# Step two's adaLN products queued behind the product that spreads the context's rstd, with priority for the context's first block

## Chip, cores and metric

The kernel runs on one core of a Trainium2 chip. The metric is the device time of one execution in microseconds (us). Engines: PE (TensorE, matmuls; PEld is its weight load), DVE (VectorE), ACT (ScalarE), POOL (GpSimd), SP (the engine that issues the loads).

## What is computed

One layer of a diffusion backbone: 256 latent tokens and 256 context tokens with 2048 features, all in float32. The part that matters here is the beginning, the modulated norm of both streams and the products with w_qkv that follow:

```python
sh1, sc1, g1, sh2, sc2, g2 = adaln(cond_lat, w_ada[i], b_ada[i])       # silu(c) @ w + b, 6 parts
h = modulate(rms_norm(x, norm_mix_g[i]), sh1, sc1)                     # x * (1 + scale) + shift
csh1, csc1, cg1, csh2, csc2, cg2 = adaln(cond_ctx, w_ada[i], b_ada[i])
hc = modulate(rms_norm(ctx, norm_mix_g[i]), csh1, csc1)
y, yc = neighbourhood_attention(h, hc, na_w_qkv[j], ..., not last)     # q, k, v = split(t @ w_qkv, 3)
x = x + g1 * y
hf = modulate(rms_norm(x, norm_ffn_g[i]), sh2, sc2)
x = x + g2 * conv_ffn(hf, ffn_w_up[i], ffn_conv_w[i], ffn_conv_b[i], ffn_w_down[i])
```

## The kernel before

Operands lie with features on the partitions, in 16 blocks of 128 features. Every product with a weight matrix is made of three matmuls of rounded halves: high weight with high input (L378), low weight with high input (L379), high weight with low input (L380). The halves of a weight tile are made from the loaded tile `wr`: `wh` on ACT (L163), `wl` on DVE (L164). The halves of the modulated input are `hh` (ACT, L452) and `hl` (DVE, L453).

The kernel begins in steps ("grains"): two steps of one block of features each, then seven of two blocks.

```python
GRAINS = [(0, 1), (1, 1)] + [(k, 2) for k in range(2, 16, 2)]
```

Step one is block 0, step two block 1, step three blocks 2 and 3, step four blocks 4 and 5. For each step `ada_step` makes shift and scale of its blocks for both streams: four groups of adaLN products, here called q0 to q3, each on its own quarter of the rows of w_ada. A group's weights come in two loads (L407) into one of four buffers `wx`; its matmuls (L413) add into a bank `ms`. Then ACT copies the sums to `ev` (L420), PE transposes them (L423), and DVE adds up the quarters and the bias (L428 to L436). `modulate` applies the result to the blocks (L447, L452, L453), and `first_products` multiplies the modulated blocks with the k columns and two groups of v columns of w_qkv. The k products add up in four banks `pj` over all steps; the v products of a step go to one of two banks `mx` and from there to `vsum` (L478 on ACT in step one, L480 on DVE afterwards). The pieces of a step's products are traced between the groups of the next step's `ada_step`.

The norm's rstd is made by `stats`: squares on ACT (L360), sums over the blocks on DVE (L365), sums over the partitions on PE (`col_sums`, L235, into an `mx` bank), rstd on DVE and POOL (L216 to L208), a diagonal matrix `xd` or `cd` (L221), a matmul with ones that spreads rstd over the partitions (L226, into an `mx` bank), and a copy `xb` or `cb` (L228). The latent stream `xl` is loaded and treated first, the context `xc` (L353) during step one: step one's latent products are traced before the context's `stats`, its context products after it.

The order on each engine is chosen by the scheduler of the framework: it plays the program through with estimated times and, whenever an engine is free, takes the ready instruction that was traced first. `tc.high_priority()` makes what is traced within it count as traced earlier. `tc.issue_after(ins)` queues what is traced within it, on the engine of `ins`, behind `ins`; it adds no wait. On the chip every engine works through its list in that order, and so does SP with its loads: a load that waits for its buffer holds up all loads behind it.

Of the kernel before, what the change touches and what calls it, by code (L numbers as in the profile page):

```python
# [15 lines left out]
P = 128  # L16
# [31 lines left out]
GRAINS = [(0, 1), (1, 1)] + [(k, 2) for k in range(2, 16, 2)]  # L48
# [6 lines left out]
def block_kernel(  # L55
# [13 lines left out]
    nc = tc.nc  # L69
# [9 lines left out]
    def ms():  # L79
        return ps.tile([P, CH], F32, tag="ms", name="ms", bufs=2)  # L80

    def mx():
        return ps.tile([P, CH], F32, tag="mx", name="mx", bufs=2)
# [13 lines left out]
    ones = cp.tile([P, P], F32, name="ones")  # L97
# [50 lines left out]

    last = []

    lows = []

    def wpair(src, k0, kn, c0, cn):
# [34 lines left out]
    def ahead():  # L188

        while plan and len(split) < 2:  # L190
            split.append((plan[0], wpair(*plan.popleft())))
# [8 lines left out]
    def rsqrt_newton(pool, v, n, name, bufs=2):  # L200

        r, t = [pool.tile([P, n], F32, tag=name + i, name=name + i, bufs=bufs) for i in "rt"]
        nc.gpsimd.tensor_tensor(out=r, in0=v, in1=mhalf[:, :n], op=ALU.pow)
        nc.vector.tensor_mul(t, r, r)
        nc.vector.scalar_tensor_tensor(
            out=t, in0=t, scalar=-0.5, in1=v, op0=ALU.mult, op1=ALU.mult
        )
        nc.vector.scalar_tensor_tensor(  # L208
            out=r, in0=t, scalar=1.5, in1=r, op0=ALU.add, op1=ALU.mult
        )  # L210
        return r

    def rstd_rows(pool, sums, name, copy):

        v = pool.tile([P, 2], F32, tag=name + "v", name=name + "v")
        nc.vector.tensor_scalar(  # L216
            out=v, in0=sums, scalar1=1.0 / D, scalar2=EPS, op0=ALU.mult, op1=ALU.add
        )
        r = rsqrt_newton(pool, v, 2, name, 1)
        dg = pool.tile([P, 2, P], F32, tag=name + "d", name=name + "d")  # L220
        diag = nc.vector.tensor_tensor(  # L221
            out=dg, in0=ident.unsqueeze(1).to_broadcast([P, 2, P]),
            in1=r.unsqueeze(2).to_broadcast([P, 2, P]), op=ALU.mult,
        )
        bp = mx()[:, :T]
        nc.tensor.matmul(bp, ones, dg.rearrange("p b t -> p (b t)"), start=True, stop=True)  # L226
        rb = pool.tile([P, T], F32, tag=name + "b", name=name + "b")
        copy(rb, bp)  # L228
        return rb, bp, diag.ins

    def col_sums(sums, parts):

        for i, sq in enumerate(parts):
            for b in range(2):
                nc.tensor.matmul(  # L235
                    sums[:, b : b + 1], sq[:, b * P : (b + 1) * P], ones[:, 0:1],
                    start=(i == 0 and b == 0), stop=(i == len(parts) - 1 and b == 1),
                    skip_group_check=True,
                )
        return sums  # L240
# [89 lines left out]
    def hl(kt, t):  # L330
        return hls[kt // (KD // 2)][:, kt % (KD // 2), t]
# [6 lines left out]
    s32 = xp.tile([P, KD, 32], F32, name="s32")  # L338
# [3 lines left out]
    xc = big.tile([P, KD, T], F32, tag="row1", name="xc")  # L342
# [7 lines left out]
    def stream(xin, src):  # L350
        for part in range(4):
            ks = slice(part * KD // 4, (part + 1) * KD // 4)
            nc.sync.dma_start(xin[:, ks, :], src.rearrange("(k p) t -> p k t", p=P)[:, ks, :])  # L353

    def stats(xin, name):

        sacc = None
        for kt in range(0, KD, 2):
            sq = xp.tile([P, 2, T], F32, tag="sq", name="sq", bufs=3)
            nc.scalar.activation(sq, xin[:, kt : kt + 2, :], AF.Square)  # L360
            if sacc is None:
                sacc = sq
            else:
                nacc = xp.tile([P, 2, T], F32, tag="sacc", name="sacc", bufs=2)
                nc.vector.tensor_add(nacc, sacc, sq)  # L365
                sacc = nacc
        sums = col_sums(mx()[:, 0:2], (sacc[:, 0], sacc[:, 1]))
        return rstd_rows(xp, sums, name, nc.vector.tensor_copy)
# [28 lines left out]
    def ada_step(b0, nb, work=()):  # L397

        ap_ = ms()
        n = 2 * nb * P  # L400
        for q in range(4):
            if q < len(work):
                work[q]()
            w = xp.tile([P, 4 * CH], F32, tag="wx", name="wx", bufs=4)[:, : 4 * n]
            for which in range(2):
                c0 = which * D + b0 * P
                load = nc.sync.dma_start(  # L407
                    w.rearrange("p (k s f) -> p k s f", k=4, s=2)[:, :, which, :],
                    w_ada[q * CH : (q + 1) * CH, c0 : c0 + n // 2].rearrange("(k p) f -> p k f", p=P),
                )  # L410
            loads.append(load.ins)
            for k in range(4):
                nc.tensor.matmul(  # L413
                    ap_[32 * k : 32 * k + 32, :n], s32[:, 4 * q + k, :], w[:, k * n : (k + 1) * n],
                    start=(q == 0), stop=(q == 3), tile_position=(0, 32 * k),
                )
        for piece in work[4:]:
            piece()
        ev = xp.tile([P, CH], F32, tag="ev", name="ev")
        nc.scalar.copy(ev[:, :n], ap_[:, :n])  # L420
        sp = ms()
        for b in range(2 * nb):
            nc.tensor.transpose(sp[:, b * P : (b + 1) * P], ev[:, b * P : (b + 1) * P], ident)  # L423
        blk = slice(b0, b0 + nb)
        spv = sp.rearrange("p (b g c) -> p b c g", g=4, c=32)
        for which, dst in ((0, shT), (1, gsT)):
            bcol = S_B + which * KD + b0
            nc.vector.tensor_reduce(  # L428
                out=dst[:, blk, :], in_=spv[:, which * nb : (which + 1) * nb, 0:2, :], axis=AX.X,
                op=ALU.add,  # L430
            )
            nc.vector.tensor_tensor(
                out=dst[:, blk, :], in0=dst[:, blk, :],
                in1=sm[:, bcol : bcol + nb].unsqueeze(2).to_broadcast([P, nb, 2]), op=ALU.add,
            )
        nc.vector.scalar_tensor_tensor(  # L436
            out=gsT[:, blk, :], in0=gsT[:, blk, :], scalar=1.0,
            in1=sm[:, S_GM + b0 : S_GM + b0 + nb].unsqueeze(2).to_broadcast([P, nb, 2]),
            op0=ALU.add, op1=ALU.mult,
        )  # L440

    def modulate(b0, nb, streams=None):

        for st, x_ in streams or ((0, xl), (1, xc)):
            t = slice(st * T, (st + 1) * T)
            for kt in range(b0, b0 + nb):
                nc.vector.scalar_tensor_tensor(  # L447
                    out=x_[:, kt, :], in0=x_[:, kt, :], scalar=gsT[:, kt, st : st + 1], in1=rb[st],
                    op0=ALU.mult, op1=ALU.mult,
                )  # L450
                sh = shT[:, kt, st : st + 1]
                nc.scalar.activation(hh[:, kt, t], x_[:, kt, :], AF.Identity, bias=sh)  # L452
                nc.vector.scalar_tensor_tensor(  # L453
                    out=hl(kt, t), in0=x_[:, kt, :], scalar=sh, in1=hh[:, kt, t].bitcast(F32),
                    op0=ALU.add, op1=ALU.subtract,
                )
# [29 lines left out]

    stream(xl, xT)
    rb = [stats(xl, "x")[0]]
    ada_step(*GRAINS[0])
    ahead()  # L490
    stream(xc, ctxT)
# [1 line left out]
    work = first_products(*GRAINS[0])  # L493
    work[0]()
    work[1]()
    rb.append(stats(xc, "c")[0])
    modulate(*GRAINS[0], ((1, xc),))
    for j, grain in enumerate(GRAINS):
        work = first_products(*grain) if j else work[2:]
        if j + 1 < len(GRAINS):  # L500
            ada_step(*GRAINS[j + 1], work)
            modulate(*GRAINS[j + 1])
        else:
            for piece in work:
                piece()
# [36 lines left out]
    def split_k(kps):  # L542
        kh = kv.tile([P, 4, 2 * T], F32R, tag="kh", name="kh")
        kl = kv.tile([P, 4, 2 * T], F32R, tag="kl", name="kl")
        for tt in range(4):
            norm_transpose(kps[tt], kg, kh, kl, tt * P)
        return kh, kl
# [132 lines left out]
    def out_of_psum(pts, dst):  # L680

        for tt, pt in enumerate(pts):
            nc.scalar.copy(dst[:, tt, :], pt)
        return [dst[:, tt, :] for tt in range(len(pts))]

    k = split_k(out_of_psum(kps, kw))
    q = split_q(out_of_psum(project(0, 2), qw))
    for g in range(3):
# [13 lines left out]
        k = split_k(kps)  # L702
        q = split_q(qps)
# [301 lines left out]
```

## Time and profile before

| | |
|---|---|
| median of 3 runs | 1408.59 us (1408.5 to 1409.4) |
| profiled execution | 1407.63 us |
| its span | 1405.8 us |
| PE busy | 1379.6 us, 98% of the span |
| DVE busy | 1027.2 us, 73% |
| ACT busy | 702.8 us, 50% |
| moved by DMA | 317.14 MB, mean 226 GB/s |

The span runs from the first to the last instruction of the program in the profiled execution; all times of the trace count from its start. The share of busy time is an average over stages; the stage of the change is the first 54 us. The line numbers are those of the kernel before.

### The profile page before, as it was taken

How to read it: one execution, taken by the hardware profiler on the slowest of the kernel's cores; microseconds unless marked ns; L12 is line 12 of the kernel's file. 1: busy time of each engine (PE TensorE's matmuls, PEld its weight loads, DVE VectorE, ACT ScalarE, POOL GpSimd, SP SyncE). 2: the span in 40 equal slices, each digit the busy share in tenths (PEclk: the TensorE clock that was granted, in tenths of full speed). 3: DMA queues.
4: the chain of work that ended last, by engine and by line, in shares of the span. 5: the costliest groups of instructions: out<-in, count | busy, mean ns of one | idle time of the engine just before them, and what ended most of it. 6: DMA issues, size and time to landing. Idle time of an engine off the chain costs nothing.

```text
span 1405.8 us, 20819 instructions
## 1 busy us (share of the span) xinstructions
PE 1379.6 (98%) x7672; PEld 1166.5 (83%) x7672; DVE 1027.2 (73%) x1694; ACT 702.8 (50%) x1218; POOL 54.8 (4%) x57
## 2 busy tenths in 40 slices
PE   4999999999999999999999999999999999999999
PEld 2565788888888888888988888888888888888888
DVE  4555678879877989789897887878878675545454
ACT  4322254564444573554675565655556564333333
POOL 1000010120010020000000000000000000000000
PEclk9999999999999999999999999999999999999999
DMA  9998737768776878656767777777776666566554
GB/s 306 357 354 288 232 95 239 228 214 257 227 243 188 275 209 277 192 189 225 241 187 250 242 227 233 234 238 237 239 238 200 179 190 206 183 208 204 171 178 145
DMA packets 208919, 317.14 MB, mean 226 GB/s; under 512 B 23360, under 2 KB 87744, under 8 KB 208816
## 3 DMA queue, kind: packets, MB, share of 16 engines
q1 hardware_dynamic: 208688, 315.79, 71.8%
q8 instruction: 60, 0.98, 0.3%
q14 instruction: 43, 0.35, 0.1%
q10 hardware_dynamic: 128, 0.01, 0.0%
HBM read 312.75 MB, written 3.01 MB: 225 GB/s over the span
## 4 chain that ended last, share of the span: by engine, by line
PE 94%; DVE 2%; DMA 2%; SPq 1%; issue 0%; ACT 0%; DVEq 0%; ACTq 0%
PE pj L734 20%; PE pj L741 10%; PE mx L734 9%; PE pj L378 8%; PE pj L379 8%; PE pj L380 8%; PE ms L734 8%; PE mx L741 5%; PE ms L741 4%; PE mx L378 2%; PE mx L379 2%; PE ms L413 2%; PE mx L380 2%; DMA wx<-in_w_ada 1%; PE ms L633 1%; DVE wl L164 1%
## 5 line engine op out<-in xcount | busy, mean ns | idle before, releaser
L164 DVE TENSOR_TENSOR wl<-wr,wh 128x1024 fp32r<-128x1024 f32 (+2 forms) x425 | 477.4, 1124 | 254.3 <-ACT wh L163 126.5
L163 ACT CAST wh<-wr 128x1024 fp32r<-128x1024 f32 (+2 forms) x425 | 413.5, 974 | 487.6 <-PE pj L734 127.8
L379 PE MATMUL pj<-wl,hh 128*128 128x512 f32 x512 | 202.6, 396 | 0.0
L380 PE MATMUL pj<-wh,hl 128*128 128x512 f32 x512 | 199.8, 392 | 0.0
L378 PE MATMUL pj<-wh,hh 128*128 128x512 f32 x512 | 193.0, 396 | 2.5 <-ACT hh L452 2.5
L280 DVE SCALAR_TENSOR_TENSOR acc<-wa,sT,acc 128x512 f32<-128x512 f32 x240 | 184.1, 769 | 1.9
L734 PE MATMUL pj<-hf,wh 128*128 128x512 f32 x624 | 146.3, 390 | 0.0
L734 PEld LDWEIGHTS pj<-hf,wh 128*128 128x128 f32 x624 | 115.6, 188 | 23.0
L378 PEld LDWEIGHTS pj<-wh,hh 128*128 128x128 f32 x512 | 95.8, 188 | 26.4 <-issue 3.4
L379 PEld LDWEIGHTS pj<-wl,hh 128*128 128x128 f32 x512 | 96.5, 188 | 21.4 <-DVE wl L164 0.9
L380 PEld LDWEIGHTS pj<-wh,hl 128*128 128x128 f32 x512 | 96.4, 188 | 18.8
L734 PE MATMUL mx<-hf,wh 128*128 128x512 f32 x352 | 94.6, 390 | 0.0
L734 PE MATMUL ms<-hf,wh 128*128 128x512 f32 x336 | 90.5, 389 | 0.0
L741 PEld LDWEIGHTS pj<-hf,wl 128*128 128x128 f32 x624 | 77.5, 192 | 1.6
L741 PE MATMUL pj<-hf,wl 128*128 128x256 f32 x624 | 78.0, 283 | 0.0
L734 PEld LDWEIGHTS mx<-hf,wh 128*128 128x128 f32 x352 | 64.7, 188 | 12.3
L734 PEld LDWEIGHTS ms<-hf,wh 128*128 128x128 f32 x336 | 63.1, 188 | 13.4
L480 DVE TENSOR_TENSOR vsum<-vsum,mx 128x512 f32<-128x512 f32 x64 | 43.1, 683 | 34.3 <-PE mx L380 34.1
L873 ACT ACTIVATE y<-z,sm 128x256 f32<-128x256 f32 x86 | 51.6, 601 | 10.6 <-DVE z L856 10.6
L413 PE MATMUL ms<-wx,s 128*32 128x512 f32 (+1 forms) x288 | 36.9, 582 | 16.3 <-DMA wx<-in_w_ada 16.3
L378 PE MATMUL mx<-wh,hh 128*128 128x512 f32 x128 | 52.7, 412 | 0.1
L379 PE MATMUL mx<-wl,hh 128*128 128x512 f32 x128 | 50.6, 395 | 0.0
(264 smaller groups left out, 2031.7 us busy)
## 6 DMA issues: line engine op xcount, KB each, us to landing
wr<-in_w_up SPq DMA_DIRECT2D x160, 512.0 KB, 4.4
wa<-in_w_ada SPq DMA_DIRECT2D x128, 512.0 KB, 5.0
wr<-in_w_qkv SPq DMA_DIRECT2D x93, 512.0 KB, 4.2
wr<-in_w_down SPq DMA_DIRECT2D x63, 512.0 KB, 4.8
wx<-in_w_ada SPq DMA_DIRECT2D x56, 512.0 KB, 8.8
wr<-in_w_o SPq DMA_DIRECT2D x24, 512.0 KB, 4.9
wr<-in_w_down SPq DMA_DIRECT2D x45, 256.0 KB, 3.1
wr<-in_w_up SPq DMA_DIRECT2D x16, 384.0 KB, 3.9
```

What stands on the lines that cost most here:

```text
L163: a = nc.scalar.copy(hi[:, :kn, :cn], w[:, :kn, :cn])
L164: b = nc.vector.tensor_tensor(out=lo[:, :kn, :cn], in0=w[:, :kn, :cn], in1=hi[:, :kn, :cn].bitcast(F32), op=ALU.subtract,)
L280: nc.vector.scalar_tensor_tensor(out=acc, in0=w[:, k, :], scalar=s, in1=acc, op0=ALU.mult, op1=ALU.add)
L378: nc.tensor.matmul(pt, hh[:, kt, ts], wh[:, k, :], start=a, stop=False)
L379: nc.tensor.matmul(pt, hh[:, kt, ts], wl[:, k, :], start=False, stop=False)
L380: nc.tensor.matmul(pt, hl(kt, ts), wh[:, k, :], start=False, stop=z)
L413: nc.tensor.matmul(ap_[32 * k : 32 * k + 32, :n], s32[:, 4 * q + k, :], w[:, k * n : (k + 1) * n], start=(q == 0), stop=(q == 3), tile_pos ...
L480: nc.vector.tensor_add(acc[:, h0 + i, :], acc[:, h0 + i, :], pr_[i])
L633: nc.tensor.transpose(tp[:, kt * P : (kt + 1) * P], pr[:, kt * P : (kt + 1) * P], ident)
L734: nc.tensor.matmul(pts[b][:, : m.shape[-1]], wh[:, k, bs], m, start=(kt == 0 and t.start == 0), stop=False,)
L741: nc.tensor.matmul(pts[b][:, : m.shape[-1]], wl, m, start=False, stop=(kt == kn - 1))
L873: nc.scalar.activation(y, z, AF.Identity, bias=sm[:, S_CB + f : S_CB + f + 1], scale=sm[:, cw + 1 : cw + 2])
```

## The change

The adaLN products of step two are queued on PE behind the matmul that spreads the context's rstd. The context's `stats` and the modulation of its first block are traced with priority. The end of `ada_step` (copy, transposes, sums) becomes a function of its own, which is traced with priority in step two. The other steps' `ada_step` and all operations stay as they are; the list `behind` is empty in step one and from step three on.

```diff
+    behind = []
...
         bp = mx()[:, :T]
-        nc.tensor.matmul(bp, ones, dg.rearrange("p b t -> p (b t)"), start=True, stop=True)
+        mm = nc.tensor.matmul(bp, ones, dg.rearrange("p b t -> p (b t)"), start=True, stop=True)
+        behind[:] = [mm.ins]
...
             loads.append(load.ins)
-            for k in range(4):
-                nc.tensor.matmul(
-                    ap_[32 * k : 32 * k + 32, :n], s32[:, 4 * q + k, :], w[:, k * n : (k + 1) * n],
-                    start=(q == 0), stop=(q == 3), tile_position=(0, 32 * k),
-                )
+            with ExitStack() as es:
+                for ins in behind:
+                    es.enter_context(tc.issue_after(ins))
+                for k in range(4):
+                    nc.tensor.matmul(
+                        ap_[32 * k : 32 * k + 32, :n], s32[:, 4 * q + k, :],
+                        w[:, k * n : (k + 1) * n], start=(q == 0), stop=(q == 3),
+                        tile_position=(0, 32 * k),
+                    )
         for piece in work[4:]:
             piece()
+        with ExitStack() as es:
+            if b0 == 1:
+                es.enter_context(tc.high_priority())
+            ada_end(ap_, b0, nb)
+
+    def ada_end(ap_, b0, nb):
+
+        n = 2 * nb * P
         ev = xp.tile([P, CH], F32, tag="ev", name="ev")
...
     rb = [stats(xl, "x")[0]]
+    behind.clear()
     ada_step(*GRAINS[0])
...
     work[1]()
-    rb.append(stats(xc, "c")[0])
-    modulate(*GRAINS[0], ((1, xc),))
+    with tc.high_priority():
+        rb.append(stats(xc, "c")[0])
+        modulate(*GRAINS[0], ((1, xc),))
     for j, grain in enumerate(GRAINS):
         work = first_products(*grain) if j else work[2:]
         if j + 1 < len(GRAINS):
             ada_step(*GRAINS[j + 1], work)
+            behind.clear()
             modulate(*GRAINS[j + 1])
```

## The prediction

> **What bounds the kernel now.** I read the page first, then the busy time by stretches, then the chain of waits, then the timeline and the loads of the first 54 us.
>
> ```profile
> span 1405.8 us, 20819 instructions
> PE 1379.6 (98%) x7672; PEld 1166.5 (83%) x7672; DVE 1027.2 (73%) x1694; ACT 702.8 (50%) x1218; POOL 54.8 (4%) x57
> DMA  9998737768776878656767777777776666566554
> ...
> core 0: us, PE busy (x) PEld busy (x) DVE busy (x) ACT busy (x) POOL busy (x), PEclk, DMA share, GB/s
> 28.00:35.30 7.30, 4.57 (x44) 2.21 (x44) 1.98 (x7) 1.52 (x4) 0.70 (x1) 1.00 1.13 320
> 12.00:53.70 41.70, 34.27 (x187) 19.23 (x188) 21.00 (x55) 17.39 (x31) 1.41 (x2) 1.00 1.11 339
> 53.70:142.00 88.30, 88.28 (x452) 55.63 (x452) 51.19 (x103) 22.92 (x36) 0.00 (x0) 1.00 1.00 328
> 142.00:560.00 418.00, 417.87 (x2034) 344.19 (x2034) 338.73 (x586) 205.43 (x459) 48.00 (x39) 1.00 0.72 222
> ```
>
> PE is the bound: busy 88.28 of 88.30 us from 53.7 to 142 and 417.87 of 418.00 after that. So what the change is worth is read before 53.7 us. There the DMA share is 1.11 (full) at 339 GB/s while PE idles 41.70 - 34.27 = 7.4 us, 7.30 - 4.57 = 2.73 of them between 28 and 35.3 us, where the change acts. The chain of waits says on what:
>
> ```profile
> 24.02 0.43 PE pj L379
> ...
> 26.58 0.36 PE mx L379
> ...
> 27.39 0.48 PE mx L380 x2
> 27.87 0.30 SPq L407
> ...
> 28.22 5.42 DMA wx<-in_w_ada
> ...
> 33.77 0.67 PE ms L413 x8
> 34.47 0.38 ACT ev L420
> ...
> 34.90 0.44 PE ms L423 x2
> ...
> 44.47 9.11 DMA wx<-in_w_ada
> 53.58 0.14 issue
> 53.72 1.06 PE ms L413 x8
> ```
>
> Columns: start, duration, what. Twice the chain runs through a load of w_ada: the last one of step two (landed at 33.64) and the load issued at 44.47, which lands at 53.58 and releases step four's first products at 53.72. The stretch's own instructions:
>
> ```profile
> 22.68 0.49 ACT L452 ACTIVATE hh<-xl,shT 128x256 fp32r<-128x256 f32 x1
> 23.08 1.72 ACT L360 ACTIVATE sq<-xc 128x512 f32<-128x512 f32 x3
> 23.22 0.79 PE L378 MATMUL pj<-wh,hh 128*128 128x512 f32 x1 [2.46 <-ACT hh L452]
> 23.81 3.87 DVE L365 TENSOR_TENSOR sacc<-sacc,sq 128x512 f32<-128x512 f32 x5
> 25.16 1.15 ACT L360 ACTIVATE sq<-xc 128x512 f32<-128x512 f32 x2 [0.36 <-DMA xc<-in_ctxT]
> 27.66 1.07 ACT L478 COPY vsum<-mx 128x512 f32<-128x512 f32 x2 [0.85 <-PE mx L380]
> 28.39 0.64 PE L413 MATMUL ms<-wx,s 128*32 128x256 f32 x8 [0.53 <-DMA wx<-in_w_ada]
> 28.96 1.05 PE L235 MATMUL mx<-ones,sacc 128*128 128x1 f32 x8
> 31.61 0.43 DVE L221 TENSOR_TENSOR cd<-ident,cr 128x256 f32<-128x256 f32 x1
> 32.00 0.64 PE L413 MATMUL ms<-wx,s 128*32 128x256 f32 x8 [1.18 <-DMA wx<-in_w_ada]
> 32.57 0.70 PE L226 MATMUL mx<-cd,ones 128*128 128x256 f32 x2
> 33.31 0.42 DVE L228 COPY cb<-mx 128x256 f32<-128x256 f32 x1 [1.28 <-PE mx L226]
> 33.77 0.48 DVE L447 SCALAR_TENSOR_TENSOR xc<-xc,gsT,cb 128x256 f32<-128x256 f32 x1
> 33.77 0.64 PE L413 MATMUL ms<-wx,s 128*32 128x256 f32 x8 [0.50 <-DMA wx<-in_w_ada]
> 34.74 0.51 ACT L452 ACTIVATE hh<-xc,shT 128x256 fp32r<-128x256 f32 x1
> 35.30 0.50 PE L378 MATMUL pj<-wh,hh 128*128 128x512 f32 x1
> ...
> 53.72 1.06 PE L413 MATMUL ms<-wx,s 128*32 128x512 f32 x8 [0.83 <-DMA wx<-in_w_ada]
> ```
>
> Before 35.30 PE holds the context's column sums (L235), the spreading product (L226) and the four groups of step two's adaLN products (L413), called q0 to q3, of which three stand here. The context's chain is L235, a few small operations, cd, L226, cb, xc, hh, and its products at 35.30.
>
> **The change part by part.** Nothing is removed or added: the same matmuls, copies and loads, in another order.
>
> *The column sums come first.* q0 is at 28.39 and L235 only behind it, at 28.96. L235 needs the last sum of squares (23.81 + 3.87 = 27.68) and a bank that the first of the two vsum copies frees (27.66 + about half of 1.07 = 28.2). With q0 out of the way L235 starts at about 28.3, 0.66 us earlier.
>
> *The spreading product.* From L235's start to cd's end it is 31.61 + 0.43 - 28.96 = 3.08 us, so cd is there at 31.38 and L226 at 31.44. Before, it was at 32.57, since q2 took PE at 32.00. Gain of this chain: 1.13 us.
>
> *The context's first block.* cb starts 33.31 - 32.57 = 0.74 after L226, xc 0.46 after cb, its hh 0.5 after xc, and PE follows hh by 35.30 - 34.74 = 0.56. Before, hh stood 0.49 behind xc's end, since the ev copy of 34.47 preceded it on ACT. Now: cb 32.18, xc 32.64, hh 33.15, products possible at 33.71.
>
> *The four groups behind L226.* From q0's start to the next matmul it is 28.96 - 28.39 = 0.57 us. q0 starts 0.70 after L226, at 32.14, and ends at 32.14 + 0.64 = 32.78; q1 and q2 end at 33.35 and 33.92. q3 can't go before its load (33.77 in both), so it runs from 33.9 to 34.5. They fill the time in which DVE and ACT make hh, so they cost nothing there; without that cover they would cost 4 x 0.57 = 2.3 us. The context's products start at 34.5 instead of 35.30, with two transposes (0.44) still to do: 35.30 - 34.94 = 0.36 us won on PE. If the transposes with their priority go first, nothing is won, as then PE waits for ev as before. I take 0.36.
>
> *What waits behind the groups.* Each group reads one of four wx buffers, and step three's loads want those buffers. SP issues in order (time, duration; the last two rows are loads with their size and the time from issue to landing):
>
> ```profile
> 30.03 0.38 SPq L143 DMA_DIRECT2D wr<-in_w_qkv  x1
> 30.50 9.88 SPq L407 DMA_DIRECT2D wx<-in_w_ada  x8
> ...
> wr<-in_w_qkv SPq DMA_DIRECT2D x1, 256.0 KB, 5.0
> ...
> sm<-in_small SPq DMA_DIRECT2D x1, 253.0 KB, 2.7
> ```
>
> The first of step three's eight loads was issued at 30.50, with q0 done at 29.03. Now it waits for q0 until 32.78, with seven more loads of its step and the next weight loads queued behind it on SP. Is the queue empty by then? The last load ahead of it (wr, issued at 30.03) lands 5.0 later, at 35.0. In a full queue 512 KB more take 0.524 MB / 339 GB/s = 1.55 us, so the wx load has to land by 36.6. A load into an empty queue took 2.7 us for 253 KB (sm, the first load of the kernel); another 259 KB add 0.8: 3.5 us. So it must be issued by about 33.05. It comes at 32.78, and I cost it at nothing, with 0.27 us of margin. Every tenth that q0 ends after 33.05 costs a tenth, since the load of 53.58 stands further back in the same queue. The bounds: margin as worked (0), or L226 not earlier than now at 32.57, q0 done at 33.91, cost 0.86.
>
> *Priority of the squares on ACT and of the sums on DVE.* A fourth square (0.40 a piece in steps of 23.08 - 22.68) may now stand ahead of the latent block's hh (22.68). That moves the first products by 0.4 from 23.22, with PE idle before them, and through the vsum copies L235 by as much: q0 ends at 33.18, cost 0.13. I take zero, the order of now; the end where all squares go first is a rival below.
>
> *Where the 0.36 us go.* PE is done earlier with what stands before 53.72 and then waits for the same load: the gap of 0.83 us becomes about 1.2. The load lands when the full queue has moved what is ahead of it, and the change moves no byte less. Nothing after it changes.
>
> Sum: -0.36 on PE, +0.36 at the wait, 0 on the loads. The profiled execution had 1407.63 us, 1.83 outside the span; the median of the three runs, 1408.59, is 0.96 above it. With no change in the span the median stays: 1408.6 us. A measurement of this kernel can tell about 0.2%, 2.8 us, from no change.
>
> **The rivals.**
>
> *The load queue drains.* The mechanism above with q0 later than 33.05: +0.1 to +0.86, so 1408.7 to 1409.5. For it: the margin is 0.27 us. Against it: the chain gains 1.13.
>
> *The wait at 53.72 goes too.* The scheduler places the loads by its own times; if step four's first wx pair comes a weight load earlier (1.55 us each in the full queue), the 0.83 vanishes and the 0.36 stay: -1.2, 1407.4. Against it: nothing in the diff touches that order. If all of the idle time of 28 to 35.3 went with it, 2.73 + 0.83 = 3.6 us, it would be 1405.0, faster by more than 0.2%; but four loads that land between 28.2 and 33.64 forbid most of that.
>
> *The squares before the latent block (slower).* Place: ACT at 22.68. If the priority puts all of the context's squares ahead of hh, hh follows the last one (25.16 + 1.15 = 26.31), the first products start at 26.85 instead of 23.22, 3.6 us late, and end at 27.87 + 3.6 = 31.5. Vsum copy, L235 and L226 follow at 31.8, 31.9 and 35.0; q0 ends at 36.35, 3.3 us past 33.05: 1411.9. It exceeds 2.8 us when q0 ends after 35.9. For it: priority names exactly these squares. Against it: they wait for xc's parts (0.36 us of such a wait at 25.16), and in that time hh is ready.
>
> *PE loses its pace.* A product took 0.43 us at 24.02, 0.36 at 26.58 and 0.24 at 27.39, though the granted clock reads 1.00: the first 3.5 us of products, from 23.22 to about 26.7, ran at half pace. Between 27.87 and 31.44 PE would now do only L235 (1.05 us). If that drops it to half pace, the groups take some 0.3 to 0.5 us more each and 3.5 us of products lose 1.7: 3.1 to 3.8 us late, less the 0.83 at 53.72: +2.3 to +3.0, 1410.9 to 1411.6. Against it: from 28 to 35.3, with 2.73 us idle, the pace stayed. The Trainium skill, "TensorE: Matmul & The Clock Gate", Part 1, says that a window of about 3.4 us of idle PE takes the clock to half, and about as long of work brings it back. The trace agrees with the way up (3.5 us from 23.22); no run here shows the way down, and by that rule the sum would be this rival's.
>
> **How the numbers follow.** Likeliest, no change (within 0.7 us, 1407.9 to 1409.3): 0.55. Drained queue: 0.12. Wait gone: 0.13. Pace lost: 0.07, half of it beyond 0.2%. Squares first: 0.07. Most of the idle time gone: 0.06. So faster 0.06, slower 0.07 + 0.03 = 0.10, same 0.84. The range from 1406.6 (wait gone, and 0.8 for what I can't bound in the order) to 1411.0 (pace lost, lower end) leaves out the squares, half of the lost pace and the large gain, 0.16.
>
> **What would show it.** Right: L235 at about 28.3 and L226 near 31.4, ahead of all four groups; the groups close together up to 34.5; the context's products before 35.0; the first load of step three issued near 32.8 and landed by 36.6; the gap before 53.7 grown from 0.83 to about 1.2. Wrong: PE's idle time before 53.7 smaller by over a microsecond with nothing given back at that load; or the DMA rate sagging after 35 us; or the latent block's products starting after 24 us; or products after 35 us at 0.43 us apiece.

## The result, and the profile after

The changed kernel takes 1414.21 us (median), against 1408.55 us for the kernel before beside it: a ratio of 1.0038, 95% interval 1.0026 to 1.0049. One of its six executions took 3543.74 us for a reason that no run shows, and the ratio is formed without it; the median of the other five is 1413.78 us, 5.2 us above the kernel before (5.7 by the median of all six, which the expectations below use). That is more than the bound of 0.2%. The profiled execution took 1414.64 us (1407.63 before). In the line numbers of the changed kernel the column sums are L238, the spreading product L228, the adaLN products L419, the products with w_qkv L381 to L383, and the loads of w_ada L410.

From the page of the changed kernel, and from its busy time by stretches (length; busy time and instructions of each engine; PE's granted clock; DMA share; GB/s):

```profile
span 1412.9 us, 20818 instructions
...
PE 1384.9 (98%) x7672; PEld 1169.6 (83%) x7672; DVE 1029.7 (73%) x1694; ACT 703.5 (50%) x1218; POOL 54.2 (4%) x57
```

```profile
core 0: us, PE busy (x) PEld busy (x) DVE busy (x) ACT busy (x) POOL busy (x), PEclk, DMA share, GB/s
...
28.00:35.30 7.30, 4.68 (x33) 2.57 (x35) 2.21 (x8) 1.58 (x3) 0.70 (x1) 0.75 0.94 254
35.30:44.00 8.70, 6.71 (x42) 3.60 (x34) 3.71 (x12) 3.39 (x7) 0.00 (x0) 0.82 0.93 301
44.00:53.00 9.00, 8.09 (x37) 5.00 (x37) 0.83 (x2) 2.02 (x4) 0.00 (x0) 0.81 1.08 359
53.00:63.00 10.00, 10.00 (x59) 4.80 (x52) 7.23 (x17) 5.05 (x9) 0.00 (x0) 1.00 1.08 357
```

The same matmuls (x7672) keep PE busy 5.3 us longer, 1384.9 against 1379.6, and its idle time grows by 1.8: together the 7.1 us of the span. It arises before 53 us. The kernel before has, for the second of these stretches:

```profile
35.30:44.00 8.70, 8.70 (x43) 5.79 (x46) 4.55 (x13) 4.55 (x9) 0.00 (x0) 1.00 1.09 346
```

Two things stand in the rows that were not there before: a granted clock of 0.75, 0.82 and 0.81 where it was 1.00, and from 28 to 44 us a DMA share of 0.94 and 0.93 where it was 1.13 and 1.09. Finer stretches show both at once:

```profile
31.00:32.00 1.00, 0.00 (x0) 0.00 (x0) 0.74 (x4) 0.00 (x0) 0.12 (x1) 0.83 1.17 290
32.00:33.00 1.00, 0.69 (x2) 0.50 (x2) 0.17 (x1) 0.00 (x0) 0.00 (x0) 0.50 1.15 320
...
34.00:35.00 1.00, 1.00 (x16) 0.46 (x12) 0.49 (x1) 0.48 (x1) 0.00 (x0) 0.50 0.13 47
35.00:36.00 1.00, 1.00 (x13) 0.40 (x9) 0.48 (x1) 0.03 (x1) 0.00 (x0) 0.50 0.26 76
```

The clock falls to 0.50 within 31 to 32 us, in which PE does nothing, and the DMA engines stand almost still from 34 to 36. What PE does there, from the timeline (start, duration, engine, line, operation, idle time before it and what ended that):

```profile
28.45 1.07 ACT L493 COPY vsum<-mx 128x512 f32<-128x512 f32 x2 [1.48 <-PE mx L383]
29.09 1.05 PE L238 MATMUL mx<-ones,sacc 128*128 128x1 f32 x8 [0.45 <-ACT vsum L493]
...
31.74 0.43 DVE L223 TENSOR_TENSOR cd<-ident,cr 128x256 f32<-128x256 f32 x1
32.31 1.19 PE L228 MATMUL mx<-cd,ones 128*128 128x256 f32 x2 [2.17 <-DVE cd L223]
33.43 3.64 PE L419 MATMUL ms<-wx,s 128*32 128x256 f32 x32
34.58 8.76 SPq L410 DMA_DIRECT2D wx<-in_w_ada  x8
37.01 0.80 PE L381 MATMUL pj<-wh,hh 128*128 128x512 f32 x1
...
41.92 1.06 PE L419 MATMUL ms<-wx,s 128*32 128x512 f32 x8 [0.97 <-DMA wx<-in_w_ada]
44.91 1.59 PE L419 MATMUL ms<-wx,s 128*32 128x512 f32 x8 [1.93 <-DMA wx<-in_w_ada]
46.43 0.80 PE L381 MATMUL mx<-wh,hh 128*128 128x512 f32 x1
```

The order is the one that the diff asks for: column sums, spreading product, four groups, context's products. But the spreading product stands at 32.31, only 0.26 us earlier than before, behind 2.17 us of idle PE, and lasts 1.19 instead of 0.70. The four groups take 3.64 us, so the context's products start at 37.01 instead of 35.30. The first load of step three waits for q0 and is issued at 34.58 instead of 30.50, so q0 and q1 of step three wait for their loads at 41.92 and 44.91. The chain of waits now runs through these places:

```profile
29.09 1.07 PE mx L238 x8
...
31.74 0.44 DVE cd L223
32.31 1.19 PE mx L228 x2
33.50 1.06 PE ms L419 x8
34.58 0.38 SPq L410
35.01 1.45 SPq L410
...
37.06 7.71 DMA wx<-in_w_ada
44.91 1.59 PE ms L419 x8
```

So it goes from the spreading product over q0 to SP, and from SP over the loads of step three to q1 of that step. Behind each of the two gaps (idle 2.17 at 32.31, 1.93 at 44.91) the next operation is slow: 1.19 instead of 0.70, and 1.59 where the same group at 41.92 took 1.06.

### The profile page after: what moved, and what is told of

Same layout as the page of the kernel before. It is cut to its first block, busy times and chain, and to the rows that moved or that the text cites. A ratio compares the mean times of both kernels' runs of the same rounds, so it can differ in the third digit from the quotient of the medians.

```text
span 1412.9 us, 20818 instructions
## 1 busy us (share of the span) xinstructions
PE 1384.9 (98%) x7672; PEld 1169.6 (83%) x7672; DVE 1029.7 (73%) x1694; ACT 703.5 (50%) x1218; POOL 54.2 (4%) x57
## 4 chain that ended last, share of the span: by engine, by line
PE 94%; DVE 2%; DMA 1%; SPq 1%; issue 0%; ACT 0%; POOL 0%; DVEq 0%; ACTq 0%
PE pj L752 20%; PE pj L759 10%; PE mx L752 9%; PE pj L382 8%; PE pj L381 8%; PE pj L383 8%; PE ms L752 7%; PE mx L759 5%; PE ms L759 4%; PE mx L381 2%; PE ms L419 2%; PE mx L382 2%; PE mx L383 2%; PE ms L651 1%; SPq L410 1%; DVE wl L166 1%
## 5 line engine op out<-in xcount | busy, mean ns | idle before, releaser
L383 PE MATMUL pj<-wh,hl 128*128 128x512 f32 x512 | 199.7, 393 | 0.0
L381 PE MATMUL pj<-wh,hh 128*128 128x512 f32 x512 | 193.5, 396 | 2.5 <-ACT hh L467 2.5
L381 PEld LDWEIGHTS pj<-wh,hh 128*128 128x128 f32 x512 | 96.3, 189 | 24.0 <-ACT hh L467 3.7
L383 PEld LDWEIGHTS pj<-wh,hl 128*128 128x128 f32 x512 | 96.5, 188 | 18.9
L419 PE MATMUL ms<-wx,s 128*32 128x512 f32 (+1 forms) x288 | 39.3, 617 | 16.1 <-DMA wx<-in_w_ada 16.1
L381 PE MATMUL mx<-wh,hh 128*128 128x512 f32 x128 | 53.7, 420 | 0.1
```

Source lines behind the costliest of these rows:

```text
L381: nc.tensor.matmul(pt, hh[:, kt, ts], wh[:, k, :], start=a, stop=False)
L383: nc.tensor.matmul(pt, hl(kt, ts), wh[:, k, :], start=False, stop=z)
L419: nc.tensor.matmul(ap_[32 * k : 32 * k + 32, :n], s32[:, 4 * q + k, :], w[:, k * n : (k + 1) * n], start=(q == 0), stop=(q == 3), tile_pos ...
```

## The experiments

Two theories came out of these traces. **Pace**: with the groups moved away PE is idle between the column sums and the spreading product, drops to half clock, and does the groups and products behind it slowly. **Queue**: the first load of step three comes too late, the load queue runs dry, and everything behind it in that queue lands later. The rival to both is **order**: the list is worse by itself (q0 and q1 of step three follow each other, and the products that stood between come later). All ratios are to the kernel before, run beside each kernel.

**Queueing alone.** e1 leaves out both priorities.

```diff
-            if b0 == 1:
-                es.enter_context(tc.high_priority())
...
-    with tc.high_priority():
-        rb.append(stats(xc, "c")[0])
-        modulate(*GRAINS[0], ((1, xc),))
+    rb.append(stats(xc, "c")[0])
+    modulate(*GRAINS[0], ((1, xc),))
```

> The groups are queued behind the spreading product; both priorities are left out. If the queueing alone makes the loss (my theory), this is the changed kernel again: about 5.5 us slower than before, the granted clock at half from about 31.6 us on. If the priorities make a part of it (rival), the loss is smaller by that part: under 4 us.

Measured: 1414.51 against 1408.16 us, 1.0039 [1.0025, 1.0053]. The whole loss is there without the priorities. The queueing on PE makes the loss; up to 66 us the instruction lists of the two programs differ in a couple of swapped neighbours only.

**Pace kept.** e2 is the changed kernel with two matmuls between the context's column sums and the spreading product, whose results nothing reads.

```diff
+    def keep_busy(n):
...
+        f = ms()
+        for _ in range(n):
+            mm = nc.tensor.matmul(
+                f, ones, xl[:, KD - 2 : KD, :].rearrange("p k t -> p (k t)"), start=True, stop=True
+            )
+        return mm.ins
...
-        mm = nc.tensor.matmul(bp, ones, dg.rearrange("p b t -> p (b t)"), start=True, stop=True)
+        with ExitStack() as es:
+            if name == "c":
+                with tc.issue_after(done[-1]):
+                    es.enter_context(tc.issue_after(keep_busy(2)))
+            mm = nc.tensor.matmul(bp, ones, dg.rearrange("p b t -> p (b t)"), start=True, stop=True)
```

> The changed kernel with two idle matmuls of 128x512 (their result is not used) between the context's column sums and the spreading product, where PE had 2.17 us of nothing. Pace theory: the clock stays at full after 28 us, the busy time of PE falls by most of the 5.3 us that it grew by, q0 ends at about 33.6 instead of 34.5, and of the loss of 5.7 us 1 to 2 us are left, those of the drained queue. Drained-queue theory (pace of no weight): the loss stays at 5 us or more, since the first load of step three still goes out after 33 us.

Measured: 1410.34 against 1408.16 us, 1.0011 [1.0002, 1.0020]. Timeline, and two of the stretches:

```profile
29.31 1.96 PE L219 MATMUL ms<-xl,ones 128*128 128x512 f32 x4
...
31.62 0.67 PE L241 MATMUL mx<-cd,ones 128*128 128x256 f32 x2 [0.35 <-DVE cd L232]
...
39.31 1.07 PE L435 MATMUL ms<-wx,s 128*32 128x512 f32 x8 [1.51 <-DMA wx<-in_w_ada]
```

```profile
28.00:35.30 7.30, 6.29 (x49) 3.38 (x50) 2.46 (x8) 1.71 (x4) 0.70 (x1) 1.00 1.03 285
...
33.00:34.00 1.00, 0.73 (x18) 0.19 (x11) 0.42 (x2) 0.51 (x1) 0.00 (x0) 1.00 0.65 226
```

Two matmuls of no use (x4 in the row: each counts twice, as the four of a group count x8) take back 3.0 of the 5.2 us; 2.2 are left. In the profiled execution the clock stays at 1.00 and the spreading product takes 0.67 instead of 1.19. The queue still sags (0.65 from 33 to 34 us), and a wait of 1.51 for step three's first load stays at 39.31. The two matmuls changed one thing more: the scheduler now puts products with w_qkv between step three's q0 and q1, which in the changed kernel follow each other. So e2 alone does not separate pace from order.

**Half of the queueing.** e3 queues q2 and q3 alone.

```diff
-                for ins in behind:
+                for ins in behind if q > 1 else ():
```

> The changed kernel, but only q2 and q3 are queued behind the spreading product; q0 and q1 go ahead of it as before. The two buffers of q0 and q1 come free at about 29 and 31 us, so the queue does not drain, and PE has work in 28 to 31 us, so the clock stays. The spreading product should start at about 32.1 instead of 32.57 us. Both theories: time within 1 us of the kernel before; if the front gains anything that the load of 53.58 us does not swallow, it is 0.4 to 1 us faster. If the order of the later groups (step three's q0 and q1 back to back, as in the changed kernel) is a cause of its own, a gap of 1 us or more before 46 us stays and the kernel is 1 to 3 us slower.

Measured: 1409.53 against 1408.16 us, 1.0010 [1.0001, 1.0019]. With q0 done early, step three's first load was issued at 31.65, while the last load ahead of it landed at 36.18, so the queue did not run dry. It is 1.4 us slower, and a gap at step three's q1, which here too follows q0 directly, is there. That is what the order rival had forecast (a gap of 1 us or more before 46 us, 1 to 3 us slower). But in the profiled execution the clock fell too, to 0.50 from 33.4 to 36.8 us and again from 43.6 to 47.1; the paragraph on the clock within one list, below, comes back to it. The gap:

```profile
42.95 1.30 PE L419 MATMUL ms<-wx,s 128*32 128x512 f32 x8 [2.00 <-DMA wx<-in_w_ada]
```

**The queue drained, in the order of before.** e4 is the kernel before with step three's loads held on SP behind a store that waits for the context's modulated block.

```diff
+    scrap = dp.tile([16, T], F32, name="scrap")
+    late = nc.sync.dma_start(scrap, xc[:16, 0, :])
...
+                    if b0 == 2:
+                        es.enter_context(tc.issue_after(late.ins))
+                    load = nc.sync.dma_start(
```

> The kernel before, with step three's loads held on SP behind a small store that waits for the context's first modulated block (about 34.3 us); the products are not queued. Only the queue is drained, as in the changed kernel, and PE keeps its groups between 28 and 34 us. Drained-queue theory: 3 to 5 us slower. Pace theory: the clock stays at full, and the loss is what the later loads cost where PE waits for them, 1.5 to 3 us.

Measured: 1411.14 against 1408.16 us, 1.0017 [1.0008, 1.0026]: 3.0 us by the medians, 2.4 by the ratio.

```profile
34.00:35.00 1.00, 0.92 (x8) 0.16 (x8) 0.48 (x1) 0.04 (x1) 0.00 (x0) 0.61 0.12 43
...
36.00:37.00 1.00, 1.00 (x4) 0.81 (x4) 0.85 (x6) 0.00 (x0) 0.00 (x0) 0.50 0.01 1
```

A drained queue (DMA share 0.12 and 0.01) costs, with step two's groups in their old places; step three's the scheduler moved behind more products, q0 to 43.59. The clock did not stay at full, as the pace theory had it: in the profiled execution it was at 0.50 from 34.2 to 37.6 us. In the four of eleven executions with a mean clock of 1.000 the median is 1410.10, so about 2 of the 3 us are there without a recorded loss of clock. Its eighth load of step three landed at 51.16, 3.3 us later than before; in the changed kernel it was 50.76, 2.9 late.

**Clock raised at the front.** e5 is the kernel before with seven matmuls of no use at its start; e6 is the changed kernel with these and those of e2.

```diff
+    even = xp.tile([P, CH], F32, name="even")
+    nc.gpsimd.memset(even, 1.0)
+    start = ms()
+    for _ in range(7):
+        nc.tensor.matmul(start, ones, even, start=True, stop=True)
```

> The kernel before, with seven idle matmuls of 128x512 on a tile of ones at the start, while PE waits for the first load (12.4 us of nothing). It asks whether PE's pace can be had early, and whether time won in front is swallowed by the loads. If the idle matmuls bring the pace to full, the latent block's products take 2.8 us instead of 4.6 and end near 26. My step that the front's gains end at the load of 53.58 us: time within 0.7 us of the kernel before. If instead PE's own work in the front sets the end: 1.5 to 2 us faster.

> The changed kernel with the idle matmuls at the start and the two between column sums and spreading product. Pace theory with the queue as second part: the spreading product near 31, q0 done by 32.4, so step three's first load goes out before 33 us and the queue does not drain; pace full throughout; what is left is the order of step three's groups. Time 0 to 1 us faster than the kernel before. If the loss that stayed with the two idle matmuls alone (1.5 us) was not the drained queue but the order, it stays: 1 to 2 us slower than before.

Measured: e5 1408.55 against 1408.20 us, 1.0001 [0.9993, 1.0010]; e6 1410.88 against 1408.20, 1.0016 [1.0007, 1.0024]. In e5 the idle matmuls came to full pace at about 8 us (four of their records took 3.62 us from 3.65 on, and 2.35 from 7.06 on), and the granted clock fell again at 14.8, ahead of the products that it was to speed up:

```profile
0.00:23.00 23.00, 14.93 (x58) 6.31 (x58) 9.45 (x24) 9.19 (x17) 4.93 (x16) 0.82 1.00 296
23.00:28.00 5.00, 4.75 (x11) 3.79 (x12) 4.45 (x8) 4.05 (x8) 0.00 (x0) 0.50 1.12 330
28.00:35.30 7.30, 6.06 (x44) 2.25 (x43) 2.41 (x8) 1.08 (x3) 0.70 (x1) 0.73 1.13 318
```

So e5 and e6 did not raise the pace of the products of 23 to 28 us, and what that would bring stays open. e6 missed both of its forecasts (0 to 1 us faster, 1 to 2 us slower). But e5 shows something else: in the order of before, half clock lasted from 14.8 to 28.5 and from 31.9 to 35.3 us, over q2, L226 and q3, and the median was that of the kernel before, whose products ran at half pace only up to about 26.7 us.

**Step three's groups spread.** e7 (on e3) and e8 (on the changed kernel) queue each group of step three behind the products traced just before it, against the rival that their standing together is the loss.

```diff
-                for ins in behind:
+                for ins in piece if b0 == 2 else behind:
...
+                mm = nc.tensor.matmul(pt, hl(kt, ts), wh[:, k, :], start=False, stop=z)
+                piece[:] = [mm.ins]
```

> As the run with q2 and q3 alone queued, and step three's groups queued each behind the products traced just ahead of it, so that they no longer stand back to back ahead of ready products. If the gap of 2.0 us at step three's q1 was made by that order, it vanishes, and with it the half pace after 43 us: time within 0.7 us of the kernel before or faster, against 1.4 us slower without it. If the load was the cause, the gap comes back at the next group.

> The changed kernel with step three's groups queued each behind the products traced just ahead of it. The first loss of pace (31.6 to 38.4 us) and the drained queue stay, the gaps of 0.97 and 1.93 us before 45 us and the second loss of pace go. Of the loss of 5.7 us 2 to 4 us stay. If the order has no part in it, the loss stays at 5 us or more.

Measured: e7 1411.72 against 1408.20 us, 1.0027 [1.0017, 1.0036]; e8 1412.73, 1.0035 [1.0022, 1.0047]. One row of each timeline:

```profile
55.96 1.60 PE L422 MATMUL ms<-wx,s 128*32 128x512 f32 x8 [2.01 <-DMA wx<-in_w_ada]
```

```profile
57.68 1.06 PE L422 MATMUL ms<-wx,s 128*32 128x512 f32 x8 [2.16 <-DMA wx<-in_w_ada]
```

Spreading won nothing measurable on e8 and cost e7 the larger part of its loss. The likely reason: the groups free their buffers later, so step four's loads are issued later, and PE waits for those. The gap moves to a later group. So breaking up the pair at 41.92 and 44.91 does not by itself mend the loss; as it also delays step four's loads, it does not show that the pair costs nothing.

**Loads in time, with and without the pace.** e9 is the changed kernel with the loads of step three's first two groups in memory of their own, which nothing else holds yet, in front of the queue's hole. e10 is the kernel before with the same memory. e11 is e9 with the two matmuls of e2.

```diff
+    room = hp.tile([P, KD // 2, 2 * T], F32, tag="hl1", name="room")
...
+            if b0 == 2 and q < 2:
+                w = room.rearrange("p k t -> p (k t)")[:, 4 * q * CH : 4 * (q + 1) * CH]
+            else:
...
+                    if b0 == 2:
+                        es.enter_context(tc.issue_after(loads[-1]))
```

> The changed kernel, but step three's first two groups load into memory of their own (that of the later blocks' hl), so their loads wait for no buffer and the queue does not drain. PE's order up to step three's groups is that of the changed kernel, so the column sums stand alone on PE again and the pace should be lost as before, near 31.6 us. Drained-queue theory: most of the loss goes, 0 to 2 us slower than the kernel before. Pace theory: the loss of pace alone costs 4 us or more. Order theory: 1.4 us stay, as with q2 and q3 alone queued.

> The control: the kernel before with the same memory of their own for step three's first two groups. Its queue was full all the time, so no theory expects a gain from the memory itself: within 1 us of the kernel before, unless the order of the loads that the scheduler now picks moves the load of 53.58 us.

> The changed kernel with both: memory of their own for step three's first two groups, and the two idle matmuls ahead of the spreading product. Queue full and pace kept: what is left of the loss is neither of the two. Drained queue and pace together as the cause: within 0.7 us of the control, or faster by up to 1 us. Order theory: 1 to 2 us slower than the control.

| | order up to step three | clock, 28 to 44 us, profiled execution | executions with a mean clock of 1.000 | step three's loads | us, against 1408.61 (first row 1408.55, second 1408.16) | ratio |
|---|---|---|---|---|---|---|
| changed | changed | halved | none of 5 | late | 1413.78 | 1.0038 [1.0026, 1.0049] |
| e2 | changed | full | 4 of 11 | a little late | 1410.34 | 1.0011 [1.0002, 1.0020] |
| e9 | changed | halved | none of 11 | in time | 1411.43 | 1.0017 [1.0008, 1.0026] |
| e11 | changed | full | 11 of 11 | in time | 1407.89 | 0.9996 [0.9987, 1.0005] |
| e10 | before | halved | 9 of 11 | in time | 1407.72 | 0.9995 [0.9987, 1.0004] |

Rows from 28 to 44 us of e9, e11 and e10, in this order:

```profile
28.00:35.30 7.30, 4.86 (x38) 2.78 (x42) 2.46 (x8) 1.21 (x3) 0.70 (x1) 0.68 1.13 316
35.30:44.00 8.70, 7.44 (x45) 4.00 (x38) 3.60 (x11) 3.39 (x7) 0.00 (x0) 0.88 1.09 353
```

```profile
28.00:35.30 7.30, 6.54 (x43) 3.67 (x45) 2.77 (x9) 1.31 (x4) 0.70 (x1) 1.00 1.15 305
35.30:44.00 8.70, 7.02 (x48) 3.98 (x40) 4.08 (x12) 4.64 (x10) 0.00 (x0) 1.00 1.09 353
```

```profile
28.00:35.30 7.30, 5.81 (x44) 2.22 (x42) 1.98 (x7) 1.43 (x4) 0.70 (x1) 0.79 1.13 315
35.30:44.00 8.70, 8.63 (x34) 6.05 (x35) 3.96 (x12) 4.03 (x9) 0.00 (x0) 0.79 1.09 351
```

The changed kernel and e9 have the same PE list up to step three's second group and differ in the loads (share 0.94 and 0.93 against 1.13 and 1.09): 5.2 us lost against 2.8. e9 and e11 differ in the two matmuls and with them in the clock (0.68 and 0.88 against 1.00; the DMA shares are alike): 3.5 us. With both mended, e11 is as fast as its control e10 and cannot be told from the kernel before.

Where the time goes is read at step three's first groups, q0 and where needed q1. The rows are of the kernel before, e10, e9 (two) and e11 (two):

```profile
38.27 1.06 PE L413 MATMUL ms<-wx,s 128*32 128x512 f32 x8
```

```profile
40.23 1.06 PE L420 MATMUL ms<-room,s 128*32 128x512 f32 x8
```

```profile
39.91 1.07 PE L426 MATMUL ms<-room,s 128*32 128x512 f32 x8
42.24 1.07 PE L426 MATMUL ms<-room,s 128*32 128x512 f32 x8 [1.26 <-DMA room<-in_w_ada]
```

```profile
39.07 1.06 PE L442 MATMUL ms<-room,s 128*32 128x512 f32 x8
...
43.40 1.07 PE L442 MATMUL ms<-room,s 128*32 128x512 f32 x8 [1.68 <-DMA room<-in_w_ada]
```

| profiled execution | first latent product | q0 of step three | between | from q0 to the end of the span |
|---|---|---|---|---|
| before | 23.22 | 38.27 | 15.05 | 1367.5 |
| e10 | 23.11 | 40.23 | 17.12 | 1366.3 |
| e9 | 22.77 | 39.91 | 17.14 | 1369.9 |
| e11 | 24.44 | 39.07 | 14.63 | 1367.9 |

The front ("between") shows the pace directly: up to q0, e9 and e11 have the same PE list but for the two matmuls, and e9 takes 2.5 us longer. With the pace kept, the changed order's front is 0.4 us shorter than that of the kernel before in these profiles, near the 0.36 of the forecast.

Behind q0 the lists differ. In e9, as in the changed kernel, q1 follows q0 directly; in e11, as in e2, products stand between. e9 waits 1.26 us for q1's load and 0.40 for the next group's, and takes 2.4 us longer from q0 on than the kernel before. So of the 3.5 us between e9 and e11 the pace is shown for 2.5, and the rest may be order.

e10's profiled execution has its clock halved for as long as e9's (0.79 twice is 7.30 x 0.21 + 8.70 x 0.21 = 3.4 us of full clock lost; e9 7.30 x 0.32 + 8.70 x 0.12 = 3.4), and its front is as long: half clock delays the front in the order of before just as much. Behind q0, e10 gets 1.2 us of it back, since hardly a wait is left there (that of 0.83 at 53.72 is gone). The sums over 28 to 63 us, of the kernel before and of e10, have PE idle for 3.72 and 1.73 us:

```profile
sum 35.00, PE 31.28 PEld 18.48 DVE 18.42 ACT 12.84 POOL 0.70; mean PE 7.82 PEld 4.62 DVE 4.60 ACT 3.21 POOL 0.18
```

```profile
sum 35.00, PE 33.27 PEld 18.71 DVE 18.43 ACT 13.07 POOL 0.70; mean PE 8.32 PEld 4.68 DVE 4.61 ACT 3.27 POOL 0.18
```

e10's median is not that of a halved clock, though: only two of its eleven executions have a mean clock below 1.000.

**The clock within one list.** Each execution has its mean granted clock on record. Where it differs between executions of one kernel, the instruction list and the loads of the program are the same, so order is no rival. The medians (in brackets the number of executions; the split was made after the runs):

| | higher clock | lower clock | longer by |
|---|---|---|---|
| kernel before, beside e1 to e11 | 0.999 or 1.000: 1408.08 (50) | below: 1409.17 (31) | 1.1 |
| e10 | 1.000: 1407.32 (9) | below: 1408.45 (2) | 1.1 |
| e2 | 1.000: 1409.70 (4) | 0.999: 1411.07 (7) | 1.4 |
| e3 | 0.999 or 1.000: 1408.62 (6) | below: 1411.15 (5) | 2.5 |
| e9 | 0.999: 1411.86 (3) | below: 1411.19 (8) | -0.7 |

e3 is the clearest: no execution of its first group takes as long as any of its second (1409.53 against 1410.40). With q1 directly behind q0 and the clock kept, e3 is about 0.5 us slower than the kernel before; so with a full queue the order of the groups costs little, and the rest of its loss goes with the clock. In the order of before, executions with a lower clock are longer too, by 1.1 us: half clock is not free there, it costs less. e9 does not fit: its times do not follow its clock. The mean does not say where in the span the clock was lost, and why e9 loses 2.8 us at every clock stays open.

So pace and queue both cost, and with both mended the loss is gone. What the order of step three's groups adds, once the front is late or the loads are, is not separated. In the changed kernel the clock is lost twice, from 31.7 to 38.5 and, behind the gap for the late load, from 45.3 to 48.7.

## Why the prediction was wrong

The forecast was 1408.6 us, no change, with 1406.6 to 1411.0 as its range; it came to 1414.2. The steps, in their order:

- *The column sums come first, at about 28.3.* They came first, but at 29.09, no earlier than before. The products ahead of them started 0.17 us later (23.39 instead of 23.22) and stayed at half clock until 28.25 instead of 26.7; the vsum copy that frees their bank began at 28.45 instead of 27.66. The step took the old times of the products as fixed, and how long the half pace lasts differs from execution to execution: in e2's profile it ended at about 26.6, and the column sums stood at 28.39. There the whole front came out nearly as forecast: the spreading product at 31.62, step three's first load issued at 32.92, the context's products at 34.56.
- *cd at 31.38, L226 at 31.44, a gain of 1.13.* From the column sums' start to cd's end it was 31.74 + 0.43 - 29.09 = 3.08, as worked; with the late start the gain is 0.26.
- *The four groups cost nothing behind the spreading product.* **This is the first step that failed.** They were priced at 0.57 apiece, the price at full clock, under the making of hh. At half clock they took 3.64 in a row, the spreading product 0.5 more, and the context's products came at 37.01, 2.5 later than the 34.5 of the forecast.
- *The load is issued at 32.78, against a deadline of 33.05.* **The second.** It came at 34.58: 0.87 from the late spreading product, the rest from the half clock in that product and in q0. The bound of 0.86 for the cost moved L226 back to 32.57 but left q0 and that product at full clock; the eighth load was 2.9 late. The deadline itself was a little generous: the load into the empty queue took 3.85 us, not the estimated 3.5. e2, whose first load was issued at 32.92, within the deadline, still sagged and had its eighth load 0.4 late.
- *The rivals.* Both that came true were named, "the load queue drains" at 0.12 and "PE loses its pace" at 0.07, each with the right place. They were priced as if only one could happen. But the second makes the first worse, since q0 is a group at half clock, and the first came back as lost pace, since PE then waits 1.93 us for a load and loses its clock at 45.3. For lost pace the terms add up to 2.9 to 3.7 us before the 0.83 comes off, where the prediction has 3.1 to 3.8. e9, with its loads in time, lost 2.8, within the +2.3 to +3.0; but its front alone took 2.5 longer than e11's, and waits for loads behind the front, which e9 has too, were no term of that sum, so the hit is partly luck. The queue was priced too low, at +0.1 to +0.86: e4 lost 3.0, about 2 of them at full clock.
- *Against lost pace: from 28 to 35.3, with 2.73 us idle, the pace stayed.* That row gave the idle time of a stretch, in pieces with q0, q1 and q2 between. In this execution the clock went down at 31.7 after 3.4 us, from 28.25, that held only 1.05 us of column sums and 0.4 of products. The Trainium skill, "TensorE: Matmul & The Clock Gate", Part 1, gives a window of about 3.4 us of idle PE for the fall. The trace agrees with the length, but not with the idleness: PE worked 1.45 us in that window, and the clock fell all the same. This was the rival that came true, and its chance of 0.07 was set too low.
- *Nothing after it changes.* Step three's first two groups moved back to wait at 41.92 and 44.91; the old wait at 53.72 is gone (PE busy 10.00 of 10.00 from 53 to 63).

Right were that PE bounds the kernel from 54 us on, that the squares keep behind the latent block (its first products at 23.39), and that the priorities cost nothing (e1 has the whole loss without them). That a gain ahead of the loads would be swallowed by the wait at 53.72 was hardly put to the test: in e11's profile the front is 0.4 us shorter than that of the kernel before and the rest 0.4 longer, as that step had it, but its list of loads is another.

## What to carry to other kernels

Before small work is moved away from a wait, ask what it did there: here PE's clock fell once it was gone, and two matmuls of no use in its place kept the clock up. A late front costs less where waits stand behind it that it can use up. Where a buffer's release holds an in-order load queue, its deadline has to stand with the slow price of the work that releases it. Two rivals that share an instruction (here q0) are priced together, not as alternatives.

## What the runs showed of the hardware that was not expected

- The granted clock changed at multiples of about 3.4 us: full 28.25 (by the pace of the products) to 31.7, half to 38.5, full to 45.3, half to 48.7 in the changed kernel. Where such a window falls differs between executions, so nearly the same list lost three windows there and two in e1's profile: with 7.30 x 0.17 + 8.70 x 0.11 + 9.00 x 0.14 = 3.5 us of clock lost against 5.1, the span was 1411.5.
- Small matmuls do not always hold the clock, though PE counts as busy with them. In e5 it fell at 14.8 us behind 3.4 us in which PE was busy for 2.37 with two groups and the column sums; in the changed kernel it fell at 31.7 behind the column sums (1.05) and 0.4 of products. The two matmuls of e2 (1.96) held it. How much work is enough is not shown: in the kernel before, the 3.4 us from 30.1 on (counted from the change of pace at 26.7) held two groups and the spreading product, 1.98 us, and the clock stayed. e5's stretches:

```profile
11.40:14.80 3.40, 2.37 (x25) 1.34 (x24) 1.41 (x3) 0.31 (x1) 0.50 (x1) 1.00 1.17 291
14.80:18.20 3.40, 1.54 (x17) 0.46 (x16) 0.91 (x4) 0.00 (x0) 0.21 (x1) 0.50 1.11 329
```

- The page's PEclk reads 1.00 ahead of the first change that is recorded: in the profiles of the kernel before and of the changed kernel, products took 0.43 us apiece from 23.2 and 23.4 on, half pace, in stretches that show 1.00.
